# Modulation products and shift bias sums of an encoder block: from GpSimd to VectorE

## The chip, the cores and the metric

The kernel runs on one core of a Trainium2 chip. The metric is the device time of one launch in microseconds (us), as the median of several runs. A core has five engines that run in parallel, each through its own queue in order: TensorE (PE: matmuls), VectorE (DVE: elementwise), ScalarE (ACT: activations and copies), GpSimd (POOL: elementwise, and some DMA issues) and SyncE (SP: here it issues nearly all loads). Semaphores order work between engines. Data lies in SBUF (128 partitions), matmul sums in PSUM.

## The reference, cut to what matters

One encoder layer on 512 tokens of width 2048. A conditioning vector c gives six modulation vectors of 2048 elements; they shift, scale and gate the two halves of the layer.

```python
mod = jax.nn.silu(c) @ w_ada + b_ada          # w_ada: 2048 x 12288
shift1, scale1, gate1, shift2, scale2, gate2 = jnp.split(mod, 6, axis=-1)
h = modulate(rms_norm(x, norm1_w), shift1, scale1)   # h * (1 + scale) + shift
p = h @ w_in                      # Fourier channels, q, k, v, o gate, i/f gates
mix = concat(fourier_mix(u_f), mlstm_bidirectional(q, k, v, gates) * sigmoid(o))
x = x + gate1 * (mix @ w_out)
h2 = modulate(rms_norm(x, norm2_w), shift2, scale2)
u = depthwise_conv(h2 @ w_up)
x = x + gate2 * ((silu(a) * v) @ w_down)
return rms_norm(x, norm_f_w)
```

All is float32. Matmul operands are split into a high and a low word, and each product is three matmuls (high x high, high x low, low x high).

## The kernel before, in words

Activations are kept transposed: 16 tiles x_t[k] of 128 channels x 512 tokens.

The modulation vectors are not computed by TensorE. Each of the six needs a 2048 x 2048 slice of w_ada times silu(c). The slice is stored so that a tile has 128 output channels on the partitions and the inputs along the row; silu(c) is broadcast to all partitions. ada_unit (L157) loads one tile (1024 or 512 columns wide) through SyncE's queue, multiplies it with silu(c), and sums along the row into one column of adaD. It has two forms: on VectorE product and sum are one scalar_tensor_tensor with an accumulator (L167), read out by a short instruction; on GpSimd there is a product alone (L169), and the sum follows as a ScalarE copy with an accumulator (L177), put off in a list "late". The argument pool picks the form; with None every second k (512 wide) goes to GpSimd. ada_cols (L180 to L189) adds the partial sums and the bias into the modulation column.

The stages, with the time at which they run:
- First column group (0 to 113 us). For each of the 16 k-tiles, scale_tile (L360) loads two 1024-wide tiles of scale1's weights, makes the column A1[k], splits x * A1[k] into words bt[k], btl[k] (L373, L374), splits a weight tile (L120, L121) and adds to the sum of squares (L381). kouter then runs 8 x 3 matmuls of 512 columns for the o channels. From k = 1 on, the second of the two products is GpSimd's.
- Second column group (113 to 231 us). 6 x 3 matmuls per k for three heads' q and k, on the unshifted words, while shift_unit (L423) computes shift1 and shift_tile (L427) replaces each word pair by that of the normalised, shifted activation. Here rb1 is the reciprocal rms of each token. For tiles 1 to 12 ("raw") the tile is formed from x (L433, GpSimd), scaled and shifted on ScalarE (L440), copied to the high word (L441), and the low word is subtracted (L442). For the other four it is formed from the words (L435, GpSimd), multiplied by rb1 (L436), and shifted (L444, L445). L449 adds the tile's part of the shift bias of q and k. GpSimd has 11 of the 32 products. Then GpSimd multiplies the eight o tiles by rb1 (L479), held behind the last product by issue_after.
- Bias and V columns (231 to 330 us). bias_units (L494) multiplies weight rows by the shift column and sums them over k, for the channels that were computed unshifted; half of the additions are GpSimd's (L507) behind a ScalarE scaling (L506), half are VectorE's (L509). TensorE does the first head's v and the gates.
- Heads and Fourier mixer (330 to 600 us), and the output projection (600 to 728 us). Between their matmuls, pace() steps ada_gen (L239) through gate1, shift2 and scale2, in 512-wide units, every second one on GpSimd. In the output projection the tiles for them are a ring of four.
- MLP and the rest (728 us on). gate2's products are VectorE's there already (ada_gen with False).

Program order is only the input: a planner simulates the instructions on a modelled timeline and reorders each engine's queue by it, except where `pinned` keeps an instruction in program order.

Of the kernel before, what the change touches and what calls it, by code (L numbers as in the profile page):

```python
# [10 lines left out]
F32 = mybir.dt.float32  # L11
F32R = mybir.dt.float32r
I32 = mybir.dt.int32
AF = mybir.ActivationFunctionType
ALU = mybir.AluOpType
# [4 lines left out]
S = 512  # L20
# [31 lines left out]
def block_kernel(ctx: ExitStack, tc: tile.TileContext, xT, vec, wada, wg, wqk, wv0, wvu,  # L52
                 wout, wup, wdown, cst, rmask, ftab, crow, cvec, outT):
    nc = tc.nc
# [38 lines left out]
    A1 = const.tile([P, KT], F32, name="A1")  # L93
# [9 lines left out]
    def vcols(n, i, w):  # L103
        return vt[:, VC[n] + i:VC[n] + i + w]

    def raw_tile(src, w, name):
        r = wp.tile([P, 1024], F32, tag="raw", bufs=4, name=name)
        nc.sync.dma_start(r[:, :w], src)
        return r
# [27 lines left out]
    def bcast_rows(ps, cols, put):  # L137

        dg = T512("dg")
        for j in range(cols.shape[1]):  # L140
            sl = slice(j * P, (j + 1) * P)
            nc.vector.tensor_scalar(dg[:, sl], ident, cols[:, j:j + 1], None, op0=ALU.mult)
            put(ps[:, sl], onesf, dg[:, sl], start=True, stop=True)


    ada = {"late": []}
# [11 lines left out]
    def ada_unit(mod, slot, k, u, w, sb, pool=None):  # L158

        if "ring" in ada:  # L160
            r = ada["ring"][k % 4]
        else:
            r = ada["p"].tile([P, w], F32, tag="ar", bufs=ada["n"], name=f"ad{mod}_{k}_{u}")
        nc.sync.dma_start(r, wada[mod, k, :, u * w:(u + 1) * w])
        part = adaD[:, slot, k, u:u + 1]
        if not ((k if w == S else u) % 2 if pool is None else pool):
            nc.vector.scalar_tensor_tensor(r, r, 1.0, sb, op0=ALU.mult, op1=ALU.mult, accum_out=part)  # L167
        else:
            ada["pool"] = nc.gpsimd.tensor_tensor(r, r, sb, op=ALU.mult)  # L169
            ada["late"].append((r, part))  # L170
            if w == S:
                ada_late(1 if "ring" in ada else 2)

    def ada_late(n):
        while len(ada["late"]) > n:
            r, part = ada["late"].pop(0)
            nc.scalar.activation(r, r, AF.Copy, accum_out=part)  # L177
# [13 lines left out]
    bt = [None] * 16  # L191
    btl = [None] * 16
# [7 lines left out]
    def side(name):  # L200
        return pss.tile([P, S], F32, tag="s", name=name)
# [5 lines left out]
    silb = pS.tile([P, D], F32, tag="silb", name="silb")  # L207
    ada.update(p=pS, n=8)
    o_t = [None] * 8
# [29 lines left out]
    def ada_gen(mods, pool, n, shared=None):  # L239

        ada.update(p=pool, n=n)
        for u in range(4):
            sb = sbp.tile([P, S], F32, tag="sb", name=f"silu{u}")
            cq = side(f"cq{u}")
            bcast_rows(cq, vcols("c", 4 * u, 4), mm)
            nc.vector.tensor_copy(sb, cq)  # L246
            for slot, (kind, m, dst) in enumerate(mods):
                for k in range(KT):
                    ada_unit(m, slot, k, u, S, sb, pool=shared)
                    if u == 3 and k == KT - 1:  # L250
                        ada_cols(dst, kind, m, slot, 0, KT, 4)
                    yield
# [94 lines left out]
    def pinned(f, *a, **kw):  # L347
        return tc.keep_in_program_order(f(*a, **kw))


    x_t = []

    def load_x(k):
        x = (pS if 8 <= k < 13 else pX).tile([P, S], F32, tag=f"x{k}", name=f"x{k}")
        pinned(nc.sync.dma_start, x, xT[k])
        x_t.append(x)
# [3 lines left out]
    def scale_tile(k):  # L360
        ak = A1[:, k:k + 1]
        for u in (range(2) if k else (1, 0)):
            ada_unit(1, 0, k, u, 1024, silb[:, u * 1024:(u + 1) * 1024], pool=u and k)
        if k == 0:
            load_x(0)
            load_consts()
        r = raw_tile(wg[k, :, 0:1024], 1024, f"wg{k}")
        if k + 1 < KT:
            load_x(k + 1)
        ada_cols(ak, "n1", 1, 0, k, 1, 2)  # L370
        t = x_t[k]
        bt[k], btl[k] = big_tiles(k)
        nc.scalar.activation(bt[k], t, AF.Copy, scale=ak)  # L373
        nc.vector.scalar_tensor_tensor(btl[k], t, ak, bt[k].bitcast(F32), op0=ALU.mult, op1=ALU.subtract)  # L374
        w = split(r, 1024, f"wg{k}")
        if k == 0:
            nc.scalar.activation(ssq1, t, AF.Square)
        else:
            sq = T512("sq")
            nc.scalar.activation(sq, t, AF.Square)  # L380
            nc.vector.tensor_tensor(ssq1, ssq1, sq, op=ALU.add)  # L381
        return w
# [39 lines left out]

    def shift_unit(k):  # L423
        for u in range(2):
            ada_unit(0, 0, k, u, 1024, silb[:, u * 1024:(u + 1) * 1024], pool=u and k % 3 < 2)

    def shift_tile(k, r):  # L427

        sk = S1[:, k:k + 1]
        t = T512("ht")  # L430
        raw = 0 < k < 13
        if raw:
            nc.gpsimd.tensor_tensor(t, x_t[k], rb1, op=ALU.mult)  # L433
        else:
            nc.gpsimd.tensor_tensor(t, bt[k].bitcast(F32), btl[k].bitcast(F32), op=ALU.add)  # L435
            nc.vector.tensor_tensor(t, t, rb1, op=ALU.mult)  # L436
        ada_cols(sk, "g", 0, 0, k, 1, 2)
        bt[k], btl[k] = big_tiles(k)
        if raw:
            nc.scalar.activation(t, t, AF.Identity, scale=A1[:, k:k + 1], bias=sk)  # L440
            nc.scalar.activation(bt[k], t, AF.Copy)  # L441
            nc.vector.tensor_tensor(btl[k], t, bt[k].bitcast(F32), op=ALU.subtract)  # L442
        else:
            nc.scalar.activation(bt[k], t, AF.Identity, bias=sk)  # L444
            nc.vector.scalar_tensor_tensor(btl[k], t, sk, bt[k].bitcast(F32), op0=ALU.add, op1=ALU.subtract)  # L445
        if k == 0:
            nc.vector.tensor_scalar(qkb, r[:, 0:256], sk, None, op0=ALU.mult)
        else:
            nc.vector.scalar_tensor_tensor(qkb, r[:, 0:256], sk, qkb, op0=ALU.mult, op1=ALU.add)  # L449

    w = g2_weights(0)
    rb1 = pX.tile([P, S], F32, tag="x0", name="rb1")
    rc1 = rstd_cols([ssq1], slice(0, S))
    qkb = pS.tile([P, 256], F32, tag="qkb", name="qkb")
    bias = const.tile([P, 14], F32, name="bias")
# [17 lines left out]
    for i, x in enumerate((7, 6, 2, 3, 4, 5)):  # L473
        r = pX.tile([P, S], F32, tag=f"x{x}", name=f"qkraw{i}")
        nc.vector.tensor_tensor(r, g_ps[i], rb1, op=ALU.mult)
        raws.append(r)
    with tc.issue_after(ada["pool"].ins):
        for i in range(8):
            nc.gpsimd.tensor_tensor(o_t[i], o_t[i], rb1, op=ALU.mult)  # L479
    v0_first = [v0_unit(u) for u in range(2)]  # L480
    pst.close()
    pA = pa.enter_context(tc.tile_pool(name="pA", bufs=1))
# [10 lines left out]
    def bias_units():  # L493
        ada.update(p=pA, n=6)  # L494

        def unit(c, w, k, acc, first, pool):
            r = pA.tile([P, S], F32, tag="ar", bufs=ada["n"], name=f"wb{k}_{c}")[:, 0:w]
            nc.sync.dma_start(r, wg[k, :, c:c + w])
            sk = S1[:, k:k + 1]
            if first:  # L500
                if pool:
                    nc.scalar.activation(acc, r, AF.Copy, scale=sk)
                else:
                    nc.vector.tensor_scalar(acc, r, sk, None, op0=ALU.mult)
            elif pool:
                nc.scalar.activation(r, r, AF.Copy, scale=sk)  # L506
                nc.gpsimd.tensor_tensor(acc, acc, r, op=ALU.add)  # L507
            else:
                nc.vector.scalar_tensor_tensor(acc, r, sk, acc, op0=ALU.mult, op1=ALU.add)  # L509

        def acc(i, w):
            return pX.tile([P, S], F32, tag=f"x{i}", name=f"sb{i}")[:, 0:w]

        def total(i, n, accs):
            cp = side("sbp")
            for m in range(n):
                for j, a in enumerate(accs):
                    mm(cp[:, m:m + 1], a[:, m * P:(m + 1) * P], onesf[:, 0:1], start=j == 0, stop=j == len(accs) - 1)
            nc.vector.tensor_copy(bias[:, i:i + n], cp[:, 0:n])

        a, b = acc(1, S), acc(6, S)
        for k in range(KT):
            unit(1280, S, k, a, k == 0, True)
            unit(0, S, k, b, k == 0, False)
            yield
        total(10, 4, [a])
        total(0, 4, [b])
        ada["bias"] = 1
        a, b = acc(1, S), acc(6, S)
        for k in range(0, KT, 2):  # L530
            unit(S, S, k, a, k == 0, True)
            unit(S, S, k + 1, b, k == 0, False)
            yield
        nc.gpsimd.tensor_tensor(a, a, b, op=ALU.add)
        total(4, 4, [a])
        ada["bias"] = 0
        yield
        yield from ada_gen([("g", 2, G1)], pA, 6)
        yield from ada_gen([("g", 3, S2), ("n2", 4, A2)], pA, 6)

    ada["g"] = bias_units()


# [456 lines left out]
    for n, (it, m) in enumerate([(0, m) for m in LAST] + [(1, m) for m in reversed(LAST)]):  # L1000
        t = HALVES[it]
# [312 lines left out]
    for b, nk in enumerate(KBLOCKS):  # L1314
        w = 2 * nk * P
        for d in range(4):
# [3 lines left out]
            for i, wt in zip(SEVEN, ws):  # L1320
                for j in range(2):
                    m = 4 * d + 2 * j
# [4 lines left out]
                    a = ps[j][BANK[i]]  # L1327
# [163 lines left out]
```

## Time and profile before

| | |
|---|---|
| runs | 2195.56 us median of 3 (2191.17 to 2200.74) |
| profiled execution | 2191.24 us, span 2189.5 us, mean granted TensorE clock 0.973 |
| PE / PEld busy | 2042.6 us (93%) / 1946.1 us (89%) |
| DVE busy | 1810.1 us (83%) |
| ACT busy | 1129.5 us (52%) |
| POOL busy | 507.6 us (23%) |
| GpSimd modulation products | 26 of 1024 columns, 71.1 us; 96 of 512 columns, 149.5 us |
| VectorE modulation products | 38 of 1024 columns, 59.3 us; 160 of 512 columns, 148.9 us |

Busy time includes time in which an instruction has started and is held up. The span runs from the first to the last instruction; the execution's own time is a little longer. A clock of 1.00 is TensorE at full speed.

### The profile page before, as it was taken

What the parts mean: (1) busy time and instruction counts of PE and PEld (TensorE: products, weight loads), DVE (VectorE), ACT (ScalarE), POOL (GpSimd) and SP (SyncE); (2) the same over time, 40 slices, a digit from 0 to 9 for tenths busy, and PEclk for the clock granted to TensorE, in tenths of its full rate; (3) what the DMA queues carried; (4) which work ended last, traced back from release to release, by engine and by line L of the source; (5) the groups of instructions that cost most, each with busy time, mean ns of one, the idle gap of its engine ahead of it and who ended that gap; (6) DMA issues with size and microseconds to landing.
All of it is one profiled execution on the core that took longest, in us unless ns stands there. A gap on an engine that the chain in (4) does not pass through costs nothing.

```text
span 2189.5 us, 38669 instructions
## 1 busy us (share of the span) xinstructions
PE 2042.6 (93%) x15036; PEld 1946.1 (89%) x15036; DVE 1810.1 (83%) x2604; ACT 1129.5 (52%) x1749; POOL 507.6 (23%) x415
## 2 busy tenths in 40 slices
PE   6986989898999979999999999999999899999996
PEld 4764889888887969999999999999999899999996
DVE  7999897887766689989899899989887678778766
ACT  4553446554444565555555554554555455555553
POOL 3447442421434201110110111110110011111134
PEclk9998999999999989999999999999999999999998
DMA  8873864644597646666666667567566897896785
GB/s 331 289 248 113 287 216 148 193 156 150 187 324 267 185 127 185 197 184 199 184 195 197 189 192 217 160 193 221 155 188 212 317 273 183 278 262 162 196 226 155
DMA packets 165436, 456.44 MB, mean 208 GB/s; under 512 B 18354, under 2 KB 22978, under 8 KB 165252
## 3 DMA queue, kind: packets, MB, share of 16 engines
q1 hardware_dynamic: 135860, 371.64, 50.4%
q0 software_dynamic: 28304, 81.28, 17.5%
q8 instruction: 118, 1.93, 0.4%
q10 hardware_dynamic: 1088, 1.05, 0.1%
q14 instruction: 66, 0.54, 0.1%
HBM read 386.52 MB, written 67.37 MB: 207 GB/s over the span
## 4 chain that ended last, share of the span: by engine, by line
PE 56%; DVE 19%; DMA 15%; issue 5%; ACT 3%; POOL 1%; SPq 0%; POOLq 0%; DVEq 0%; ACTq 0%
DMA ad<-wada 5%; DVE ad L167 5%; DMA ring<-wada 2%; DMA gkept<-gh 2%; DMA dn_0g<-wdown 1%; PE N L628 1%; DMA mov<-gkept 1%; DMA wb<-wg 1%; PE dz L283 1%; PE dz L282 1%; PE dz L284 1%; DVE A L183 1%; PE wo L284 1%; PE wo L282 1%; PE wo L283 1%
## 5 line engine op out<-in xcount | busy, mean ns | idle before, releaser
L1332 POOL DMA_DIRECT2D xkept<-cr x80 | 69.8, 1007 | 379.7 <-DVE cr L1137 362.8
L169 POOL TENSOR_TENSOR ad<-ad,silu 128x512 f32<-128x512 f32 x60 | 96.7, 1626 | 195.2 <-DVE silu L246 152.9
L167 DVE SCALAR_TENSOR_TENSOR ad<-ad,silu 128x512 f32<-128x512 f32 x125 | 116.5, 944 | 28.5 <-DMA ad<-wada 28.2
L169 POOL TENSOR_TENSOR ad<-ad,silb 128x1024 f32<-128x1024 f32 x26 | 71.1, 2738 | 80.1 <-DMA ad<-wada 62.1
L1199 ACT ACTIVATE u<-cr,cvt 128x512 f32<-128x512 f32 x88 | 71.6, 815 | 33.1 <-DVE cr L1135 31.5
L177 ACT ACTIVATE ad<-ad 128x512 f32<-128x512 f32 (+1 forms) x86 | 64.9, 755 | 43.3 <-POOL ad L169 43.1
L1248 POOL DMA_DIRECT2D gkept<-gh x38 | 29.8, 784 | 222.3 <-ACT gh L1243 171.5
L169 POOL TENSOR_TENSOR ring<-ring,silu 128x512 f32<-128x512 f32 x36 | 52.8, 1468 | 84.1 <-DMA ring<-wada 84.1
L1201 DVE SCALAR_TENSOR_TENSOR u<-cr,cvt,u 128x511 f32<-128x511 f32 x88 | 65.5, 746 | 0.5 <-ACT u L1199 0.5
L1202 DVE SCALAR_TENSOR_TENSOR u<-cr,cvt,u 128x511 f32<-128x511 f32 x88 | 65.5, 745 | 0.0
L167 DVE SCALAR_TENSOR_TENSOR ad<-ad,silb 128x1024 f32<-128x1024 f32 x38 | 59.3, 1562 | 7.4 <-DMA ad<-wada 7.4
L177 ACT ACTIVATE ring<-ring 128x512 f32<-128x512 f32 x36 | 22.7, 631 | 61.1 <-POOL ring L169 61.0
L1243 ACT ACTIVATE gh<-gst 128x1024 fp32r<-128x1024 f32 (+1 forms) x38 | 36.0, 947 | 29.8 <-DMA gkept<-gh 24.5
L1246 DVE TENSOR_TENSOR gst<-gst,gh 128x1024 fp32r<-128x1024 f32 (+1 forms) x38 | 41.4, 1089 | 11.2 <-ACT gh L1243 11.2
L167 DVE SCALAR_TENSOR_TENSOR ring<-ring,silu 128x512 f32<-128x512 f32 x35 | 32.4, 935 | 21.1 <-DMA ring<-wada 21.1
L283 PE MATMUL dz<-mov,dz_0h 128*128 128x256 f32 (+1 forms) x156 | 48.1, 309 | 0.0
L284 PE MATMUL dz<-mov,dz_0l 128*128 128x256 f32 (+1 forms) x156 | 48.0, 308 | 0.0
L282 PE MATMUL dz<-mov,dz_0h 128*128 128x256 f32 (+1 forms) x156 | 47.9, 307 | 0.0
L628 PE MATMUL N<-v,ph 128*128 128x258 f32 x160 | 34.3, 298 | 13.9 <-DVE es L611 7.8
L507 POOL TENSOR_TENSOR sb<-sb,wb 128x512 f32<-128x512 f32 x22 | 34.5, 1569 | 44.7 <-ACT wb L506 39.8
L284 PE MATMUL wo<-mov,wo_0l 128*128 128x512 f32 x104 | 41.7, 401 | 2.8 <-DVE wo_0l L121 2.8
L284 PE MATMUL wo<-mov,wo_8l 128*128 128x512 f32 x104 | 41.7, 403 | 2.0 <-DVE wo_8l L121 2.0
(4045 smaller groups left out, 9788.0 us busy)
## 6 DMA issues: line engine op xcount, KB each, us to landing
ad<-wada SPq DMA_DIRECT2D x185, 256.0 KB, 4.1
ad<-wada SPq DMA_DIRECT2D x64, 512.0 KB, 6.4
mov<-gkept SPq DMA_DIRECT2D x52, 512.0 KB, 10.2
xkept<-cr POOLq DMA_DIRECT2D x80, 256.0 KB, 6.0
ring<-wada SPq DMA_DIRECT2D x71, 256.0 KB, 4.5
wo<-wout SPq DMA_DIRECT2D x32, 512.0 KB, 5.2
wb<-wg SPq DMA_DIRECT2D x48, 256.0 KB, 4.4
dz<-wdown SPq DMA_DIRECT2D x26, 384.0 KB, 3.5
```

The lines of the kernel that those rows point to most:

```text
L167: nc.vector.scalar_tensor_tensor(r, r, 1.0, sb, op0=ALU.mult, op1=ALU.mult, accum_out=part)
L169: ada["pool"] = nc.gpsimd.tensor_tensor(r, r, sb, op=ALU.mult)
L177: nc.scalar.activation(r, r, AF.Copy, accum_out=part)
L282: mm(ps, wh[:, sl], rh[k], start=st, stop=False)
L283: mm(ps, wh[:, sl], rl[k], start=False, stop=False)
L284: mm(ps, wl[:, sl], rh[k], start=False, stop=sp)
L628: mm(np_[:, 0:258], l[:, sl], v[:, r, t, :], start=i == 0, stop=i == n - 1)
L1199: nc.scalar.activation(u, r, AF.Identity, bias=cv(3, ch), scale=cv(1, ch))
L1201: nc.vector.scalar_tensor_tensor(u[:, 1:S], r[:, 0:S - 1], cv(0, ch), u[:, 1:S], op0=ALU.mult, op1=ALU.add)
L1202: nc.vector.scalar_tensor_tensor(u[:, 0:S - 1], r[:, 1:S], cv(2, ch), u[:, 0:S - 1], op0=ALU.mult, op1=ALU.add)
L1246: nc.vector.tensor_tensor(lo, part, hi.bitcast(F32), op=ALU.subtract)
L1332: nc.gpsimd.dma_start(xkept[4 * d + 2 * j + r], rows[j][r], accum_op=ALU.add)
```

## The change

All modulation products go to VectorE (pool=False at the three places that choose), and with them the ScalarE summing passes go. The tile "ht" of shift_tile is formed on VectorE: for raw tiles in one operation x * A1[k] * rb1, and ScalarE then writes the shifted high word at once, without the pass between. All the shift bias units go to VectorE. The eight products of o with rb1 stay on GpSimd; issue_after, which named the last GpSimd product, gives way to `pinned`.

```diff
@@ ada_gen
-                    ada_unit(m, slot, k, u, S, sb, pool=shared)
+                    ada_unit(m, slot, k, u, S, sb, pool=False)
@@ scale_tile
-            ada_unit(1, 0, k, u, 1024, silb[:, u * 1024:(u + 1) * 1024], pool=u and k)
+            ada_unit(1, 0, k, u, 1024, silb[:, u * 1024:(u + 1) * 1024], pool=False)
@@ shift_unit
-            ada_unit(0, 0, k, u, 1024, silb[:, u * 1024:(u + 1) * 1024], pool=u and k % 3 < 2)
+            ada_unit(0, 0, k, u, 1024, silb[:, u * 1024:(u + 1) * 1024], pool=False)
@@ shift_tile
         if raw:
-            nc.gpsimd.tensor_tensor(t, x_t[k], rb1, op=ALU.mult)
+            nc.vector.scalar_tensor_tensor(t, x_t[k], A1[:, k:k + 1], rb1, op0=ALU.mult, op1=ALU.mult)
         else:
-            nc.gpsimd.tensor_tensor(t, bt[k].bitcast(F32), btl[k].bitcast(F32), op=ALU.add)
+            nc.vector.tensor_tensor(t, bt[k].bitcast(F32), btl[k].bitcast(F32), op=ALU.add)
             nc.vector.tensor_tensor(t, t, rb1, op=ALU.mult)
...
-        if raw:
-            nc.scalar.activation(t, t, AF.Identity, scale=A1[:, k:k + 1], bias=sk)
-            nc.scalar.activation(bt[k], t, AF.Copy)
-            nc.vector.tensor_tensor(btl[k], t, bt[k].bitcast(F32), op=ALU.subtract)
-        else:
-            nc.scalar.activation(bt[k], t, AF.Identity, bias=sk)
-            nc.vector.scalar_tensor_tensor(btl[k], t, sk, bt[k].bitcast(F32), op0=ALU.add, op1=ALU.subtract)
+        nc.scalar.activation(bt[k], t, AF.Identity, bias=sk)
+        nc.vector.scalar_tensor_tensor(btl[k], t, sk, bt[k].bitcast(F32), op0=ALU.add, op1=ALU.subtract)
@@ after the second group
-    with tc.issue_after(ada["pool"].ins):
-        for i in range(8):
-            nc.gpsimd.tensor_tensor(o_t[i], o_t[i], rb1, op=ALU.mult)
+    for i in range(8):
+        pinned(nc.gpsimd.tensor_tensor, o_t[i], o_t[i], rb1, op=ALU.mult)
@@ bias_units
-            unit(1280, S, k, a, k == 0, True)
+            unit(1280, S, k, a, k == 0, False)
...
-            unit(S, S, k, a, k == 0, True)
+            unit(S, S, k, a, k == 0, False)
```

## Rows read from the trace of the kernel before

**Rows 1.** Windows: start:end, length, busy us (instructions) by engine, clock, DMA share, GB/s.
```profile
0.00:113.00 113.00, 89.55 (x341) 67.39 (x342) 98.30 (x127) 53.14 (x81) 46.53 (x21) 0.97 0.84 301
113.00:231.00 118.00, 90.65 (x375) 72.25 (x375) 115.15 (x161) 50.06 (x80) 68.78 (x33) 0.88 0.55 182
231.00:330.00 99.00, 90.45 (x651) 86.02 (x650) 85.42 (x114) 49.78 (x81) 47.92 (x31) 0.97 0.79 264
330.00:600.00 270.00, 247.55 (x1764) 232.45 (x1764) 214.84 (x498) 140.28 (x320) 87.51 (x54) 0.97 0.51 164
600.00:728.00 128.00, 123.29 (x575) 102.56 (x575) 87.78 (x132) 57.83 (x108) 50.25 (x34) 0.97 0.87 298
```

**Rows 2.** Timeline of VectorE in the first group: start, duration, engine, line, operation.
```profile
76.92 1.21 DVE L167 SCALAR_TENSOR_TENSOR ad<-ad,silb 128x1024 f32<-128x1024 f32 x1
...
78.06 2.34 DVE L183 TENSOR_TENSOR A<-adaD 128x1 f32<-128x1 f32 x1
...
81.88 0.68 DVE L381 TENSOR_TENSOR ssq<-ssq,sq 128x512 f32<-128x512 f32 x1
82.48 0.74 DVE L374 SCALAR_TENSOR_TENSOR mov<-x,A,mov 128x512 fp32r<-128x512 f32 x1
```

**Rows 3.** Timeline of GpSimd, first group and end of the second.
```profile
77.71 2.67 POOL L169 TENSOR_TENSOR ad<-ad,silb 128x1024 f32<-128x1024 f32 x1 [3.06 <-DMA ad<-wada]
...
203.14 14.16 POOL L479 TENSOR_TENSOR o<-o,rb 128x512 f32<-128x512 f32 x8
```

**Rows 4.** Chain of waits in the first group: start, us, what.
```profile
25.69 8.91 DMA ad<-wada
...
58.27 1.15 DVE ad L167 x2
...
95.69 1.14 DVE ad L167 x2
```

**Rows 5.** Timeline of TensorE in the first group; seven matmuls lie between the two.
```profile
65.97 0.39 PE L237 MATMUL g<-mov,wg6l 128*128 128x512 f32 x1
...
67.78 0.39 PE L237 MATMUL g<-mov,wg6l 128*128 128x512 f32 x1
```

**Rows 6.** Groups of VectorE instructions, 113 to 231 us: busy us, mean ns, idle before.
```profile
L167 DVE SCALAR_TENSOR_TENSOR ad<-ad,silb 128x1024 f32<-128x1024 f32 x21 | 32.0, 1526 | 0.0
L449 DVE SCALAR_TENSOR_TENSOR qkb<-wh,S,qkb 128x256 f32<-128x256 f32 x15 | 15.5, 1034 | 0.2
L442 DVE TENSOR_TENSOR mov<-ht,mov 128x512 fp32r<-128x512 f32 x12 | 13.6, 1130 | 0.0
L183 DVE TENSOR_TENSOR S<-adaD 128x1 f32<-128x1 f32 x16 | 12.2, 760 | 0.0
L186 DVE SCALAR_TENSOR_TENSOR S<-S,vt 128x1 f32<-128x1 f32 x16 | 10.0, 623 | 0.2
```

**Rows 7.** Single lines: shortest/median/longest ns, first and last start.
```profile
L167 DVE SCALAR_TENSOR_TENSOR ad<-ad,silb x38: 1210/1219/3433, 8.4 to 210.7; 128x1024 f32<-128x1024 f32 x38
L449 DVE SCALAR_TENSOR_TENSOR qkb<-wh,S,qkb x15: 472/484/2632, 126.0 to 220.7; 128x256 f32<-128x256 f32 x15
L442 DVE TENSOR_TENSOR mov<-ht,mov x12: 678/684/1768, 159.1 to 221.1; 128x512 fp32r<-128x512 f32 x12
L183 DVE TENSOR_TENSOR S<-adaD x17: 146/158/2350, 118.1 to 584.2; 128x1 f32<-128x1 f32 x16, 128x16 f32<-128x16 f32 x1
L186 DVE SCALAR_TENSOR_TENSOR S<-S,vt x17: 145/159/2323, 118.2 to 700.2; 128x1 f32<-128x1 f32 x16, 128x16 f32<-128x16 f32 x1
```

**Rows 8.** Window of GpSimd's instructions on the tiles "ad", columns as in rows 1.
```profile
113.00:231.00 118.00, 24.79 (x9) 0.88 0.55 182
```

**Rows 9.** Waits, 330 to 600 us (PE) and 600 to 728 us: us, times, longest.
```profile
PE N L628 <- DVE es L611: 7.8, 5, 2.4
...
POOL ring L169 <- DMA ring<-wada: 78.0, 32, 5.9
...
DVE ring L167 <- DMA ring<-wada: 18.4, 13, 4.3
```

## The prediction

> **What bounds the kernel now.** I read the page first (TensorE busy 93% of the span, VectorE 83%, GpSimd 23%), then cut the part that the change touches into stretches: first column group, second column group, bias and V columns, heads and Fourier, output projection [rows 1]. After 728 us nothing changes engine. From 231 us on TensorE is the fullest engine of each stretch (91 to 96% busy). The first two differ: VectorE is busy 98 of 113 us and 115 of 118 us, TensorE only 90 and 91. So VectorE sets the pace of the second group. For the first the chain of waits shows the same: the VectorE product of one tile follows that of the last by (95.69 - 58.27) / 6 = 6.24 us [rows 4].
>
> Then the timeline, to see what fills a tile on VectorE. At 76.92 its own product takes 1.21 us. At 78.06 an addition of 128x1 elements takes 2.34 us [rows 2], where the shortest of that line takes 0.146 us [rows 7]. GpSimd's product ran from 77.71 to 80.38 [rows 3], and VectorE's addition ended at 80.40. So VectorE stood for 2.2 us while GpSimd multiplied, and counted as busy. The reader is to see that "busy" here is partly a hold: what GpSimd does for VectorE, VectorE pays for by waiting, and longer than the 1.14 us (76.92 to 78.06) that one product occupies it. For 512 columns the hold is 1.768 - 0.678 = 1.09 us at its longest for the subtraction of L442 [rows 7], against 0.60 us that one VectorE operation of that width occupies (81.88 to 82.48) [rows 2].
>
> **The change part by part.**
> *First group.* 15 of the 16 second products go from GpSimd to VectorE, each 1.14 us instead of a hold of 2.2 us; a hold falls in nearly every tile. VectorE's tile becomes 6.24 - 2.2 + 1.14 = 5.2 us. That is below what is late next: a tile has 8 x 3 = 24 matmuls, one every (67.78 - 65.97) / 8 = 0.226 us [rows 5], so TensorE needs 5.43 us. The transfers allow it too: their share is 0.84 at 301 GB/s, so the same bytes at a full share need 113 x 0.84 = 95 us [rows 1]. From about 35 us on (before that the chain runs through transfers, up to 34.6 us [rows 4], in which the products hide), some 12.5 tiles gain 6.24 - 5.43 = 0.8 us: 10 us. VectorE, TensorE and transfers then lie within some 8% of each other, so I take 8. Bounds: nothing, if the loads keep today's rate; 14 us, if TensorE kept up with 12.5 x 1.1.
> *Second group.* Freed: GpSimd runs 33 operations here [rows 1], 9 of them products 1024 wide [rows 8]. At 2.2 and 1.09 us of hold that is 9 x 2.2 + 24 x 1.09 = 46 us. From the other side, five groups alone show 21 x (1.526 - 1.210) + 15 x (1.034 - 0.472) + 12 x (1.130 - 0.678) + 16 x (0.760 - 0.146) + 16 x (0.623 - 0.145) = 38 us above their shortest [rows 6, 7], and smaller groups are not in it. I take 46, since the two views differ by about what is left out. But the eight rstd products on the o columns stay on GpSimd. They ran at the end of this stretch (14.16 us from 203.14) [rows 3]; pinned, with nothing before them on GpSimd's queue, they start as soon as rstd is there, near the middle of the stretch. Still the same stretch: 8 x 1.09 = 9 us of hold stays. Added to VectorE: 9 products x 1.14 and 16 forming operations of "ht" x 0.60, together 20 us. The raw tiles' subtraction becomes a three-operand one of the same width, and no more is put down for it. Net 46 - 9 - 20 = 17 us. TensorE has only 6 x 3 x 16 = 288 matmuls, 65 us, in 118 us, so it follows VectorE; I take 16. Bounds: 38 - 9 - 20 = 9 and 25, the latter if the holds of the eight fall where VectorE waits anyway. The chain on ScalarE (one pass fewer per raw tile, no summing pass per product) gets shorter and hides entirely.
> *Bias sums, 231 to 330 us.* The 22 additions on GpSimd and their scalings on ScalarE (24 with the first of each sum) become 24 VectorE operations of 512 columns, one every 0.6 to 0.7 us: 16 us added, at most 22 x 1.09 = 24 us of hold freed. VectorE has 13 us idle, TensorE 8.5 [rows 1]. The waits for their loads now all stand in VectorE's queue, ahead of the V splits. I take 0, bounds -5 (faster) to +6.
> *Later modulations, 330 to 728 us.* 54 and 34 GpSimd operations [rows 1] become VectorE ones of 0.6 us, a little more with their accumulator read, 33 and 21 us, against holds of at most 59 and 37. So VectorE gets no fuller than 215 of 270 and, in the worst case (no hold freed), 109 of 128 us. TensorE is idle 22 us in the first of these, 7.8 of them behind the score products on VectorE [rows 9], and 5 in the second: I take 3 us of gain. The cover here is VectorE's idle time, 55 and 40 us; the price if it goes is a rival below.
>
> Sum: 8 + 16 + 0 + 3 = 27 us. The profiled execution took 2191.24 us (span 2189.5), so 2164 us on its scale; the median of the three runs shown, 2195.56, lies 4.3 us above it, so I forecast 2168.
>
> The Trainium skill, Perfetto Trace Analysis, section Optimizing Scalar/DVE Operations, says that work may move off a saturated VectorE, even to GpSimd, though the two share a port and it "might not help". By its first half this change goes the wrong way, since it brings work to the engine that is busy 98% of the second group, and the sum would be that of rival D. By the rows the caveat decides, as far as they go: the 128x1 additions that take 2.3 us beside a GpSimd product show the hold.
>
> **The rivals.**
> *A, more is gained.* The freed VectorE also closes TensorE's gaps after 231 us: 7.8 us behind the score products [rows 9], half of the 8.5 us in the bias stretch, and the second group gives 25. For it: VectorE's short operations in the heads are stretched by products. Against: much of the idle time there waits for other things. 8 + 25 + 12 = 45 us: 2151.
> *B, no change.* The first group is held by its loads at today's 301 GB/s and gives nothing; the second gives its lower bound, 9 us, since products now wait for loads in VectorE's queue with the weight splits behind them. For it: the loads' share of 0.84. Against: the lower rate may be the slow return of the buffers, which wait today for a second engine and a third. 2195.6 - 9 = 2187.
> *C, slower: loads waited for in the output projection.* There GpSimd waited 78.0 us for ring loads over 32 products, 2.4 us each, and VectorE 18.4 us over its own [rows 9], about as many since k alternates between the two. Both now stand in one in-order queue, and behind a product that waits stand the low halves of the output weights, for which TensorE waits. If each of the 34 moved products keeps 2.4 us, VectorE gets 34 x (2.4 + 0.61) = 102 us more in a stretch with 40 us of idle; less at most 20 of hold freed, 42 us are lost, and 24 are gained before: 18 slower, 2214. It decides from the point where a moved product waits (40 + 20 - 21) / 34 = 1.1 us, and it turns the sign at 1.1 + 24 / 34 = 1.9 us. Against it: VectorE's own products wait 18.4 / 34 = 0.54 us, GpSimd's mostly because it had nothing else to do, and a ring slot is released earlier without the summing pass.
> *D, slower: the busy time is work.* VectorE is the bound of the second group; if the long operations are long for a reason of their own, nothing is given back, and the first group's 15 x 1.14 = 17 us and the second's 20 us are paid in full: 2195.6 + 37 = 2233. The Trainium skill's advice on a saturated VectorE, above, is this case. Against it: an addition of 128x1 elements cannot be 2.3 us of work, and it ended 0.02 us after GpSimd's product.
>
> **How the numbers follow.** Forecast 0.58 (its own range 2156 to 2181), A 0.20, B 0.13, C 0.06, D 0.03. The range 2146 to 2190 takes in A and B and leaves C, D and a little of A out. A measurement of this kernel can tell 0.5%, 11 us, from no change, so below 2184.6 counts as faster: the forecast and A, 0.79 with a share of B. Same 0.13, slower 0.08 (C and D, less a part of C near zero).
>
> **What would show it.** Right: the VectorE products of the first group follow each other at 5.4 to 5.7 us; no 128x1 operation of L183 or L186 over 0.3 us save beside the eight products on o; the second group's matmuls end some 24 us earlier; VectorE's total busy time falls although it has 122 products and some 40 other operations more; ScalarE falls by 80 us or more. Wrong: a tile period that stays near 6.2 us with VectorE now idle before its product (B), VectorE waiting over 60 us for ring loads with TensorE idle in the output projection (C), or operations as long as before without GpSimd beside them (D). It would also be wrong if the planner's order, which it draws anew, puts the weight splits behind the new products.

## The result and the profile after

The changed kernel takes 2128.68 us (median of four runs, 2123.46 to 2129.73), the kernel before 2197.09 in the same comparison: a ratio of 0.9686, 95% interval 0.9659 to 0.9714. It is 68 us faster. The forecast said faster, but by 27 us, and the lower end of its range was 2146: the size was wrong. The profiled execution after took 2123.46 us, the one before 2191.24.

The page after, first two lines (busy us and share of the span by engine):

```profile
span 2121.7 us, 38452 instructions
...
PE 2017.6 (95%) x15036; PEld 1931.7 (91%) x15036; DVE 1769.0 (83%) x2888; ACT 1020.3 (48%) x1469; POOL 221.6 (10%) x255
```

VectorE has 2888 instructions instead of 2604 (162 operations and 122 short accumulator reads more) and is busy 41 us less. TensorE does the same 15036 matmuls in 25 us less.

To see where the 68 us went, the stretches are cut anew: the two groups and the output projection end with their last matmul (the first group at 124.0 us before, not at 113), the bias and V stretch where the first head's products of scores and v begin (tile N). Columns as in [rows 1]. The kernel before:

```profile
13.30:124.00 110.70, 96.77 (x385) 75.30 (x386) 104.68 (x134) 55.79 (x89) 49.72 (x19) 0.97 0.87 309
124.00:228.40 104.40, 77.05 (x307) 60.54 (x306) 102.20 (x134) 40.18 (x64) 65.39 (x32) 0.87 0.51 167
228.40:330.20 101.80, 93.17 (x673) 88.62 (x671) 88.22 (x124) 51.25 (x84) 47.92 (x31) 0.97 0.78 259
...
330.20:754.00 423.80, 396.72 (x2554) 361.01 (x2555) 316.36 (x662) 211.68 (x454) 143.36 (x96) 0.98 0.62 204
```

The kernel after:

```profile
13.60:103.40 89.80, 89.80 (x385) 74.15 (x386) 87.34 (x174) 37.90 (x54) 0.00 (x0) 1.00 1.01 387
103.40:190.90 87.50, 73.53 (x308) 58.95 (x306) 84.59 (x159) 24.59 (x33) 14.09 (x8) 0.92 0.55 182
190.90:286.20 95.30, 94.21 (x711) 90.27 (x710) 88.72 (x167) 34.66 (x51) 2.15 (x1) 1.00 0.83 288
...
286.20:690.90 404.70, 387.70 (x2518) 354.71 (x2517) 309.21 (x836) 151.39 (x271) 5.02 (x8) 0.98 0.64 213
```

| stretch | before | after | gained | forecast |
|---|---|---|---|---|
| first group | 110.7 | 89.8 | 20.9 | 8 |
| second group | 104.4 | 87.5 | 16.9 | 16 |
| bias and V columns | 101.8 | 95.3 | 6.5 | 0 |
| heads and output projection | 423.8 | 404.7 | 19.1 | 3 |

That is 63.4 of the span's 67.8 us. A second profile of the changed kernel (below) gives 20.6, 15.3, 7.3 and 16.8, together 60.0. The reader is to see two things in TensorE's column. Its idle time in the four stretches (length less busy) falls from 13.9 + 27.4 + 8.6 + 27.1 = 77 us to 0 + 14.0 + 1.1 + 17.0 = 32 us. And its busy time falls by 18.5 us for the same matmuls (some 37 of the last stretch run in the third now), with the granted clock at 0.92 instead of 0.87 in the second group and at 1.00 instead of 0.97 in the first and third: before, part of the matmuls between gaps ran at the lower level of 1.2 GHz. (A matmul at the edge of a gap also counts with its full 0.39 us instead of 0.226, so the 18.5 us are not the clock's alone.)

The first group is now TensorE's. Its chain of waits, from 40 to 103 us, holds no other engine; tiles follow each other at 49.01 - 43.57 = 5.44 us:

```profile
43.57 1.81 PE g L235 x8
49.01 1.81 PE g L235 x8
```

Single lines after (shortest/median/longest ns), against [rows 7]:

```profile
L183 DVE TENSOR_TENSOR A<-adaD x17: 149/158/179, 11.3 to 556.8; 128x1 f32<-128x1 f32 x16, 128x16 f32<-128x16 f32 x1
...
L186 DVE SCALAR_TENSOR_TENSOR S<-S,vt x17: 145/150/175, 95.8 to 641.2; 128x1 f32<-128x1 f32 x16, 128x16 f32<-128x16 f32 x1
...
L167 DVE SCALAR_TENSOR_TENSOR ad<-ad,silb x64: 1212/1218/2306, 8.7 to 171.5; 128x1024 f32<-128x1024 f32 x64
```

The 128x1 operations of these lines, up to 2.35 us before, now take at most 0.18 us. One long product is left (2.306 us). It stands beside the eight products of o, which GpSimd still does:

```profile
127.24 14.09 POOL L348 TENSOR_TENSOR o<-o,rb 128x512 f32<-128x512 f32 x8 [126.80 <-DVE S L183]
```

VectorE's timeline in the same 14 us: five operations that take 0.74 us each elsewhere take 8.58.

```profile
133.31 8.58 DVE L433 SCALAR_TENSOR_TENSOR ht<-x,A,rb 128x512 f32<-128x512 f32 x5
```

And the rival that VectorE would wait for ring loads has not come: 16.8 us in the output projection, against 18.4 before [rows 9].

```profile
DVE ring L167 <- DMA ring<-wada: 16.8, 17, 2.2
```

### The profile page after: what moved, and what is told of

It reads as the page before. It is cut to its first block, busy times and chain, and to the rows that moved or that the text cites. A ratio compares the mean times of both kernels' runs of the same rounds, so it can differ in the third digit from the quotient of the medians.

```text
span 2121.7 us, 38452 instructions
## 1 busy us (share of the span) xinstructions
PE 2017.6 (95%) x15036; PEld 1931.7 (91%) x15036; DVE 1769.0 (83%) x2888; ACT 1020.3 (48%) x1469; POOL 221.6 (10%) x255
## 4 chain that ended last, share of the span: by engine, by line
PE 66%; DMA 15%; DVE 13%; issue 3%; ACT 2%; POOL 1%; SPq 0%; POOLq 0%; DVEq 0%; ACTq 0%
DMA ad<-wada 4%; DVE ad L167 3%; DMA ring<-wada 2%; DMA gkept<-gh 2%; PE un L320 1%; PE un L318 1%; PE un L319 1%; PE g L235 1%; PE g L236 1%; PE g L237 1%; PE N L622 1%; PE wo L283 1%; PE wo L284 1%; PE wo L282 1%; PE vn L318 1%
## 5 line engine op out<-in xcount | busy, mean ns | idle before, releaser
L167 DVE SCALAR_TENSOR_TENSOR ad<-ad,silu 128x512 f32<-128x512 f32 x185 | 122.2, 686 | 17.8 <-DMA ad<-wada 17.4
L167 DVE SCALAR_TENSOR_TENSOR ad<-ad,silb 128x1024 f32<-128x1024 f32 x64 | 78.7, 1235 | 7.8 <-DMA ad<-wada 7.7
L167 DVE SCALAR_TENSOR_TENSOR ring<-ring,silu 128x512 f32<-128x512 f32 x71 | 47.2, 688 | 17.1 <-DMA ring<-wada 16.8
L282 PE MATMUL wo<-mov,wo_8h 128*128 128x512 f32 x104 | 40.8, 399 | 1.5 <-ACT mov L793 1.5
L283 PE MATMUL wo<-mov,wo_8h 128*128 128x512 f32 x104 | 41.3, 398 | 0.8 <-DVE mov L794 0.7
L282 PE MATMUL wo<-mov,wo_0h 128*128 128x512 f32 x104 | 40.6, 391 | 0.0
L283 PE MATMUL wo<-mov,wo_0h 128*128 128x512 f32 x104 | 40.6, 390 | 0.0
L120 ACT ACTIVATE dz_0h<-dz 128x768 fp32r<-128x768 f32 x26 | 22.0, 845 | 30.4 <-PE dz L283 23.6
```

The source lines that it names most:

```text
L282: mm(ps, wh[:, sl], rh[k], start=st, stop=False)
L283: mm(ps, wh[:, sl], rl[k], start=False, stop=False)
```

## The experiments

Theory H: GpSimd's products cost the time by holding VectorE up. Rivals: the load buffers came back late through a second and a third engine, or ScalarE's summing passes stood in the way (B, A); the planner's new order made the difference (O, P, S). These letters are the experiments' own: A and B of the prediction are other rivals. "Longer" is against the changed kernel, whose medians were 2128.68 and, run again, 2128.85.

**The first group's products alone, on the kernel before.**

```diff
-            ada_unit(1, 0, k, u, 1024, ..., pool=u and k)
+            ada_unit(1, 0, k, u, 1024, ..., pool=False)
```

> The kernel before, with only the first group's 15 second products moved to VectorE. Theory H (a GpSimd operation that reads SBUF holds VectorE up, so in group 1 the products on GpSimd cost VectorE 2.2 us of standing each, from the first tile on): the group's 384 matmuls end at 103 to 106 us instead of 124, and the whole is 18 to 22 us shorter than before, about 2176. Rival O (the gain in group 1 comes from the planner's new order over the whole kernel, not from these products): less than 10 us shorter, 2187 or more.

2174.87 us, ratio to before 0.992 (0.9891 to 0.9949): 22 us shorter. The first group, window as above:

```profile
13.30:103.00 89.70, 89.52 (x385) 73.65 (x386) 87.90 (x158) 38.80 (x56) 9.08 (x4) 1.00 0.97 372
```

110.7 became 89.7, the same as with the whole change; the second group took 105.5, against 104.4. The first term belongs to these 15 products, whatever the rest of the order is. (The profiled run was the longest of nine, 2187.01 us. In it the later stages took some 17 us more than in the kernel before, so the row speaks for the first group and the median for the whole.)

**GpSimd work that nobody reads, in the first group.**

```diff
+        if 0 < k:
+            for j in range(2):
+                nc.gpsimd.tensor_tensor(idle, t, silb[:, j * S:(j + 1) * S], op=ALU.mult)
```

> The changed kernel, with two extra GpSimd multiplications of 128x512 per tile in the first group (x times silu(c) into an unused buffer) whose result nobody reads; VectorE's order there is the same. Theory H: two holds of 1.1 us per tile come back, VectorE has about 2.5 us of idle time in the group, so the group gets 15 x 2.2 - 2.5 = 30 us longer (tile period about 7.3 us instead of 5.4) and the whole 25 to 32 us: 2153 to 2161. Rival B (what cost time was the slow return of the load buffers through GpSimd and ScalarE): nothing waits for these operations, so less than 5 us: 2124 to 2134.

2159.42 us, 31 longer. The group took 120.2 us, 30.4 more, against the 30 worked out:

```profile
13.40:133.60 120.20, 100.32 (x385) 78.78 (x386) 118.94 (x174) 37.58 (x54) 52.87 (x30) 0.91 0.85 288
```

GpSimd's timeline there, and VectorE's beside it:

```profile
63.16 3.39 POOL L377 TENSOR_TENSOR idle<-x,silb 128x512 f32<-128x512 f32 x2 [4.61 <-DMA x<-xT]
```

```profile
63.55 1.24 DVE L189 TENSOR_TENSOR A<-A,vt 128x1 f32<-128x1 f32 x1
...
65.32 2.31 DVE L167 SCALAR_TENSOR_TENSOR ad<-ad,silb 128x1024 f32<-128x1024 f32 x1
```

A 128x1 product takes 1.24 us instead of 0.16 and the 1024-wide one 2.31 instead of 1.21, one hold of 1.1 us for each of the two GpSimd operations. VectorE's order in the group is unchanged and no operation waits for the result, so the hold is shown as such. The Trainium skill, SBUF — State Buffer, section Who interferes with whom, calls the port pair that GpSimd shares with VectorE an exclusive lock, and says that a VectorE instruction with two SBUF inputs contends for it with a GpSimd operation that reads SBUF. Both VectorE rows are of that kind and are held, which agrees; the 1.1 us are these rows' own.

**Products on VectorE, sums still on ScalarE.**

```diff
-            ada["pool"] = nc.gpsimd.tensor_tensor(r, r, sb, op=ALU.mult)
+            nc.vector.tensor_tensor(r, r, sb, op=ALU.mult)
```

(with the old values of pool, so that 122 products take this form)

> The changed kernel, but the 122 moved products are VectorE products without accumulator, and their sums stay ScalarE passes as before; GpSimd has none of them. Theory H: only the engine of the product counts, group 1 ends within 3 us of 103.4 and the whole within 6 us of the changed kernel, 2124 to 2135. Rival B (slow buffer return, ScalarE's passes): half or more of group 1's 20 us and some of the later gain are given back, 2142 or more.

2149.78 us, 21 longer. Theory H misses. Rival B has the whole right (2142 or more) but not the place: group 1 does not give back half of its 20 us.

```profile
13.30:107.40 94.10, 91.16 (x385) 74.80 (x386) 89.72 (x162) 55.94 (x87) 0.00 (x0) 0.98 1.00 382
```

In the first group 4.3 of 21 us return; all kernels here whose work in it is the changed kernel's took 89.6 to 90.1, so this is clear. The second group and the bias stretch together take 184.9 instead of 182.8 (work moved from one to the other), heads and projection 411.4 instead of 404.7. But other kernels with the changed kernel's work in the last of these took 401.2 to 410.6 there, so where the later price lies is not shown. From the first group's end to the projection's this kernel takes 596.3 us, against 587.5 and 590.6 in the two profiles of the changed one. So the sums' way through ScalarE had a price of its own, some 10 to 13 us over the stretches in this profile, the fastest run of four (2141.91); the rest is not explained by it.

**The later modulations back on GpSimd.**

```diff
-                    ada_unit(m, slot, k, u, S, sb, pool=False)
+                    ada_unit(m, slot, k, u, S, sb, pool=shared)   # None: every second k
```

> The changed kernel, with the 96 products of gate1, shift2 and scale2 back on GpSimd for every second k. Theory H: the gain of the heads (11 us) and of the output projection (8 us) is theirs, 12 to 20 us of it returns: 2141 to 2149. Rival S (those stages gained by starting in another order, or by the granted clock): less than 6 us returns, 2135 or less.

2160.62 us, 32 longer, more than any theory said. Heads and projection:

```profile
289.20:714.90 425.70, 395.23 (x2528) 357.87 (x2529) 313.84 (x660) 209.90 (x452) 145.19 (x96) 0.98 0.62 203
```

The 19 us are lost again (21), and 3.7 more before them, where the first of these products run. The remaining 7 us of the medians' difference are not explained by these stretches; after 715 us the two kernels do the same.

**GpSimd work that nobody reads, in the later stages.**

```diff
+                    if m < 5 and k % 2:
+                        for j in range(2):
+                            jk = tiny.tile([P, DV], F32, tag="jk", bufs=1, name="jk")
+                            nc.gpsimd.tensor_tensor(jk, sb[:, j * DV:(j + 1) * DV],
+                                adaD[:, slot, k, u:u + 1].to_broadcast([P, DV]), op=ALU.mult)
```

> The changed kernel, with two extra GpSimd multiplications of 128x256 behind every second product of gate1, shift2 and scale2 (96 products); they read silu(c) and the product's column, nobody reads what they write, and no load buffer waits for them. Theory H (of the 21 to 24 us that the later stages gained by these products, most is the hold): bias, heads and projection together 10 to 18 us longer than in the changed kernel, about 2142. Rival B (most is the buffers' return through a second and a third engine): less than 4 us, 2125 to 2133.

2146.89 us, 18 longer:

```profile
285.40:707.60 422.20, 392.47 (x2517) 357.33 (x2517) 356.60 (x839) 148.47 (x266) 167.67 (x195) 0.96 0.63 205
```

422.2 us against 404.7 and, in the second profile of the changed kernel, 407.0: 15 to 17 us return without a load buffer being held. VectorE's busy time in the stretch rises by 47 us though it has the same work. So the hold alone costs time here. GpSimd is busy 168 us in this stretch and was 143 before the change, and VectorE has the moved products beside the hold (busy 357 us, 316 before). The dose is thus not the one before, and that the hold accounts for most of the 19 is likely, not shown.

**ScalarE work that nobody reads, at the same places.**

```diff
+                            nc.scalar.activation(jk, sb[:, j * DV:(j + 1) * DV], AF.Copy,
+                                scale=adaD[:, slot, k, u:u + 1])
```

> The changed kernel, with two extra ScalarE copies of 128x256 at the same places, as long together as one summing pass, again read by nobody and holding no load buffer. Keeping the summing passes gave 9 us back in these stages. Theory A (ScalarE's time in front of the splits' high halves costs that): 4 to 9 us longer, about 2135. Rival B (a load buffer that goes through a second engine comes back later): less than 3 us, 2125 to 2132.

2135.28 us, 6 longer, which by the whole would be theory A. The stretch does not show it:

```profile
286.60:692.90 406.30, 389.78 (x2516) 356.35 (x2515) 309.26 (x836) 236.27 (x456) 4.69 (x7) 0.97 0.64 212
```

406.3 us, between the two profiles of the changed kernel, with ScalarE busy 85 us more. No price of ScalarE's time shows in this stretch, though kernels with the same work there spread over 9 us (401.2 to 410.6), so one of a few us is not excluded. That leaves the buffers' return as the likelier price of the late sums, argued by exclusion and not shown. The 6 us of the medians do not lie in this stretch; behind 693 us this kernel does the same as the changed one.

**The changed kernel again.**

> The changed kernel itself, once more, as the measure for the three others on the same chip. All theories: 2123 to 2133 us, as in its first four runs. What it is also for: after 691 us (up projection and later) nothing that the change touches runs, so if the 6 us by which that part was shorter in the first profile come and go between runs, they are not the change's.

2128.85 us. What it is for, from the output projection's end to the down projection:

```profile
694.30:1640.00 945.70, 910.29 (x7438) 903.44 (x7437) 844.08 (x1100) 521.03 (x692) 98.07 (x121) 0.98 0.63 187
```

945.7 us, as before the change (945.3), where the first profile had 938.8. Over all kernels here this part took 938.8 to 950.1. So the last 4 us of the difference between the two spans are not shown to be the change's, and effects of some 6 us are read from the stretches, not from the whole. In the first two groups and the bias stretch kernels with the same work agree within 2 us, in heads and projection only within 9.

**Half of the bias sums back.**

```diff
-            unit(1280, S, k, a, k == 0, False)
+            unit(1280, S, k, a, k == 0, True)
-            unit(S, S, k, a, k == 0, False)
+            unit(S, S, k, a, k == 0, True)
```

> The changed kernel, with half of the shift bias sums back on ScalarE and GpSimd. The forecast's step (added work and freed hold cancel, TensorE is the bound): within 4 us of the changed kernel. Theory H (the bias and V stretch gained its 6.5 us from these sums, whose holds stretched the short gate operations): 5 to 9 us longer, about 2135.

2137.86 us, 9 longer, and the stretch takes 102.5 instead of 95.3:

```profile
191.10:293.60 102.50, 95.70 (x690) 91.18 (x689) 90.61 (x143) 49.27 (x74) 36.67 (x23) 0.95 0.80 267
```

The sums moved were worth 7 us, not 0: kernels with the changed kernel's work in this stretch took 94.5 to 95.6.

**The second group back.** All of the kernel before in shift_unit, shift_tile and the products of o; the rest as changed.

> The changed kernel, with the second group as before: 11 products, the forming of ht and the ScalarE passes back, the products on o behind them. Theory H: group 2 takes 104 us instead of 87.5, the rest is as in the changed kernel, 14 to 19 us longer: 2143 to 2148. Rival O (the stretch got shorter mostly since loads came earlier from the shorter first group): less than 8 us longer.

2142.02 us, 13 longer, just under theory H's 14 and far over rival O's 8; the group takes 105.8 us, about as before the change (104.4), though the first group ends early:

```profile
103.20:209.00 105.80, 81.30 (x307) 62.72 (x306) 104.20 (x140) 41.56 (x66) 66.28 (x32) 0.87 0.52 171
```

**The products of o out of the second group.** First by moving them to VectorE, behind the first bias sums in program order:

```diff
-    for i in range(8):
-        pinned(nc.gpsimd.tensor_tensor, o_t[i], o_t[i], rb1, op=ALU.mult)
...
+        for i in range(8):
+            nc.vector.tensor_tensor(o_t[i], o_t[i], rb1, op=ALU.mult)
         ada["bias"] = 1
```

> The changed kernel, with the last eight GpSimd products (o times rstd) taken out of the second group: they are done on VectorE after the first bias sums, in the bias and V stretch. Theory H (each holds VectorE 1.1 us in a group that VectorE fills): group 2 gets 7 to 10 us shorter (87.5 to about 79), the next stretch at most 3 longer (8 x 0.6 us on a VectorE with 6 us idle, TensorE full), the whole 4 to 9 us shorter than the changed kernel. Rival P (the second group's matmuls wait because the planner put weight splits behind other VectorE work): less than 3 us.

2127.57 us: no difference. The planner drew them forward into the second group (85.2 us), so it did not test what it was made for. Then with a column from the bias sums (value 1) as a factor, which makes them wait:

```diff
+        nc.vector.tensor_scalar(one, bias[:, 10:11], 0.0, 1.0, op0=ALU.mult, op1=ALU.add)
+        for i in range(8):
+            nc.vector.scalar_tensor_tensor(o_t[i], o_t[i], one, rb1, op0=ALU.mult, op1=ALU.mult)
```

> As e4_o_late (the eight products o times rstd on VectorE after the first bias sums), but each also multiplies by a column made from those sums (value 1), so that the planner can't draw them forward into the second group as it did there. Theory H: no GpSimd operation is left in the second group, its 9 us of hold go and VectorE's 5 us come due in the bias stretch, where TensorE is full and VectorE has 6 us idle: the group takes 78 to 81 us instead of 87.5 to 89, the next stretch up to 4 longer, the whole 4 to 9 us shorter than the changed kernel, about 2122. Rival: the group's length is set by VectorE's work in order, and what is freed is lost in the next stretch: less than 3 us in all.

2124.06 us, ratio to before 0.9665 (0.964 to 0.969). Second group and bias stretch:

```profile
103.40:182.20 78.80, 71.06 (x307) 57.59 (x306) 75.85 (x159) 24.08 (x33) 0.00 (x0) 0.96 0.61 201
```

```profile
182.20:285.90 103.70, 103.05 (x785) 99.10 (x784) 96.68 (x178) 35.90 (x52) 1.37 (x1) 1.00 0.80 274
```

The group gives up its last hold, 8.7 us. The next stretch gets 8.4 longer, where theory H said up to 4, but with TensorE full and 74 matmuls more, which heads and projection then lack (400.2 instead of 404.7 us). Its median is the lowest of all, 4.6 below the changed kernel; the intervals of the two ratios overlap, so it is not shown to be faster.

**The weight splits first.**

```diff
+        inorder[0] = k > 5
+        s = split(r[:, :768], 768, f"wh{k}")
+        inorder[0] = False
```

> The changed kernel, with the second group's weight splits from k = 6 on kept in program order, so that the planner can't put them behind later VectorE work. Theory P (the group's 14 us of TensorE waiting for low halves are an effect of the order): TensorE's waits for them fall to under 5 us, the group gets 5 to 9 us shorter, the next stretch longer by what was put off, up to 4: 3 to 7 us shorter in all, about 2124. Theory H (VectorE is full in the group, 84 of 87 us, whatever the order): the work put off comes due before the V columns, less than 2 us in all.

2131.45 us, the group 87.9 us against 87.5 and 89.1:

```profile
102.80:190.70 87.90, 73.09 (x308) 58.77 (x306) 84.32 (x158) 24.41 (x33) 13.71 (x8) 0.92 0.56 184
```

TensorE's waits moved to other tiles. VectorE is full in this group (busy 84 of 88 us), and this change of its order made no difference; theory P falls.

## Why the prediction was wrong in size

The mechanism was right, and so was the side; three terms were too small.

*First group, 8 forecast, 21 measured.* The step that failed is that before 35 us "the chain runs through transfers, up to 34.6 us [rows 4], in which the products hide". It read a chain ending on a landing as a limit of transfers. The kernel before, TensorE's wait by releaser in the first 60 us (L373 writes the high word, which needs the column A1[k] from VectorE):

```profile
PE g L235 <- ACT mov L373: 9.3, 4, 3.7
```

After, no such wait is left in the group. Two windows of before and then of after show the same rate of loads at first, but another from 37.5 us on:

```profile
25.00:37.50 12.50, 10.96 (x41) 8.28 (x41) 11.45 (x11) 5.43 (x9) 7.99 (x3) 0.86 1.03 406
37.50:50.00 12.50, 8.78 (x33) 6.78 (x31) 11.45 (x13) 4.70 (x7) 5.62 (x3) 0.86 0.69 257
```

```profile
25.00:37.50 12.50, 12.50 (x56) 10.34 (x56) 12.07 (x25) 6.31 (x9) 0.00 (x0) 1.00 1.03 405
37.50:50.00 12.50, 12.50 (x57) 10.34 (x56) 12.40 (x25) 4.39 (x6) 0.00 (x0) 1.00 1.03 405
```

With the same bytes landing by 37.5 us TensorE had 56 matmuls to run instead of 41. The loads ran ahead into their buffers, and the tiles stood behind held VectorE operations from the second tile on. VectorE's timeline before, where these operations otherwise take 1.21 and 0.75 us:

```profile
20.07 3.40 DVE L167 SCALAR_TENSOR_TENSOR ad<-ad,silb 128x1024 f32<-128x1024 f32 x1
...
24.73 2.62 DVE L374 SCALAR_TENSOR_TENSOR mov<-x,A,mov 128x512 fp32r<-128x512 f32 x1 [0.79 <-ACT mov L373]
```

By 50 us TensorE had run 103 matmuls before and 156 after; at 0.226 us each that is 12 of the 21 us. The floor of 5.43 us for a tile was right (5.44), but it held for all 16 tiles, and the last 2 us that were taken off for three engines close together were not needed.

*Second group, 16 forecast, 17 measured.* Right: 46 us of hold less 9 kept less 20 added. VectorE's busy time in the group fell by 17.6 us (102.20 to 84.59), and the 9 us that were kept are shown by the last hold's removal (8.7). The hold and the shorter ScalarE chain were put back together, not one by one; that ScalarE's part hides is argued from its 40 busy us of 104. The sum was worked out for 113 to 231 us, which takes in the last 11 us of the first group.

*Bias sums, 0 forecast, 7 measured.* The step that set 16 us of added work against at most 24 of freed hold and took 0 counted VectorE's time and not what waits for it. TensorE's 8.6 us of idle time there were waits for gate and score operations on VectorE (am 3.8, gt 2.6, es 2.2 us), and with the holds gone one of 1.1 us is left. That each of them was stretched by a hold is argued from the first group's rows; the sums' part is shown.

*Later modulations, 3 forecast, 19 measured.* The step that failed took less than half of one wait, the 7.8 us behind the score products, as the whole gain; putting the products back on GpSimd lost 21 us in these stages. Idle time of TensorE in the last two stretches fell by 17.6 us together (35.7 to 18.1), and TensorE's busy time for the same matmuls by 8 us more, part of it clock (1.00 instead of 0.97 in the bias stretch); the prediction had taken that time for fixed work. Rival A named these gaps and gave them 12 us, and with 45 us in all it fell short too.

*Rivals.* B (loads at 301 GB/s) fell: the loads went to 405. C fell: VectorE's products, the moved ones among them, wait 16.8 us for 71 ring loads, 0.24 each, far below its point of 1.1. D fell with the idle GpSimd work. The signs named beforehand all came (tile period, no 128x1 operation over 0.3 us, VectorE's busy time down with 162 operations more, ScalarE 109 us less) save that the second group's matmuls ended 37.5 us earlier, not 24.

*Left open.* How the 10 to 13 us of the late sums divide between load buffers and ScalarE was tested in the later stages alone, where the spread is as large as their part. That the 4 us behind 691 us are chance is likely from their spread, not shown.

## What to carry to other kernels

An engine's busy time can contain another engine's work: look for a tiny operation that takes microseconds, see what ran beside it, and price an offload by what it holds up, not by what it takes over. A wait that ends on a landing says that the load came last, not that loads are the limit; compare the rate in that window with the highest rate of the trace. And a freed gap of TensorE can give back more than its length: here 45 us less idle time came with 18.5 us less busy time for the same matmuls, part of it because matmuls beside the gaps had run at the lower clock.

## What the runs showed that was not expected

Loads held 405 GB/s for 75 us in the first group (a share of 1.03 in each of six windows from 12.5 to 87.5 us), where the prediction had worked with 358 from 301 GB/s at 0.84. And GpSimd multiplications whose results nobody reads made the changed kernel 18 us (192 of them, later stages) or 31 us (30 of them, first group) longer.
